# Dilated-attention scores on 128 rows, in column halves of 64 queries

## The chip, the cores and the metric

One core of a Trainium2 chip runs the whole program. The metric is the device time of one execution in microseconds (us), taken as the median of several runs. Besides, one execution was recorded by the hardware profiler; every duration below is from that one.

## What is computed

A hybrid encoder layer on two inputs, a "sample" of 1024 tokens and a "prompt" of 256 tokens, all in float32. Cut to what matters here:

```python
h = _rmsnorm(x, g_mix)
z = h @ w_in                      # queries, keys, values of both branches, gates
o_a = _banded_attention(qa, ka, va, A_WINDOW, 1, rel_bias[:, :A_HEADS], sink)
o_b = _dilated_mixture(qb, kb, vb, rel_bias[:, A_HEADS:])   # the branch that is changed
merged = gates0 * (o_a @ w_branch_a) + gates1 * (o_b @ w_branch_b)
x = x + merged @ w_out
y = _rmsnorm(x + square(relu(_rmsnorm(x, g_mlp) @ w_up)) @ w_down, g_final)
```

In the dilated branch there are three groups (window, dilation) = (128, 1), (512, 4), (2048, 16) of four heads, each head 64 wide. For every query the scores are `q . k / 8 + bias(distance)` over the keys of its window, then softmax and a sum over the values; the three groups are joined by their log-sums. The bias comes from a table of 32 buckets by heads.

## The kernel before, in words

The large products (`six`, L347; `mm3`, L191) are split by hand into high and low parts in the type float32r and use the full array: 128 rows of contraction by 128 columns of weights. The first stage projects the input. It runs over `PAIRS`, 14 pairs of 128 output columns; `pair` (L924) makes one of them with seven block products, and between pieces of about 12 matmuls it calls `tick` (L982). The small work of the dilated branch is laid between these pieces: every few ticks the generator `attention_b` (L489) makes one turn. The order of instructions on every engine is the order in which the code issues them (a manual schedule).

`BATCHES` (L475) cuts the dilated branch into 48 batches, by group and pair of heads. There are three kinds:

- 24 "wide" batches: one tile of 128 queries against 256 keys;
- 12 "double" batches: two tiles of 128 queries against 128 keys each;
- 12 "two-piece" batches: one tile whose first 64 queries and last 64 queries meet different stretches of 128 keys.

Turn j of `attention_b` issues, in this order (L581 to L590): the transposes of batch j-1 (L556), the values product of batch j-2 (L570), the scores of batch j (L537), the loads of values for j and of queries and keys for j+2 (L503, L505, on SP's queue). The first two turns have no values product, and the last two have no scores.

A batch covers two heads. Head 0 lies in partitions 0 to 63 of the tile `qk`, head 1 in partitions 64 to 127 (`HALVES`), so a scores matmul contracts over 64 rows: its weights are 64 rows by 128 queries (64 by 64 in a two-piece batch). The values product uses 128 rows by 64 columns: each half of the queries is a matmul of its own. Every plain float32 matmul shows as two instructions in the trace, each with its weight load. After the scores, VectorE adds the bias and takes the maximum (L541), and ScalarE the exponential (L545). `qk` has three buffers.

The generator `line` (L286) makes one row of bias for each of six cases: it loads a one-hot table of 33 rows on POOL's queue (L291), multiplies it with the bias table `tab` (33 rows by 20 heads, L295) into 256, 384 or 512 columns, and writes the result out over POOL's queue. Its steps are spread over a `pair` as hooks.

SP's queue also carries the weights of the next pair (`raw`, L377), the stores of finished pieces (L848) and the values (L519), all in the order of issue.

Of the kernel before, what the change touches and what calls it, by code (L numbers as in the profile page):

```python
# [10 lines left out]
F32 = mybir.dt.float32  # L11
# [4 lines left out]
P = 128  # L16
# [7 lines left out]
AH = 8  # L24
BH = 4
FF = 4 * D
EPS = 1e-6
NEG = -1e30
BUCKETS, MAXD = 32, 1024
# [20 lines left out]
HALVES = (slice(0, HD), slice(HD, P))  # L50
# [46 lines left out]
def encoder_kernel(  # L97
# [5 lines left out]
    nc = tc.nc  # L103
# [15 lines left out]
    const = ctx.enter_context(tc.tile_pool(name="const", bufs=1))  # L119
# [15 lines left out]
    def bank(tag, name=None):  # L135
        return psum.tile([P, 512], F32, name=name or tag, tag=tag, bufs={"mm": 3, "sc": 2, "pt": 2, "pv": 1}[tag])
# [115 lines left out]
    nc.vector.memset(eps, EPS)  # L252
    bg = const.tile([P, 2 * KC], F32, name="bg")
    nsink = const.tile([P, AH], F32, name="nsink")
    tab = const.tile([BUCKETS + 1, AH + 3 * BH], F32, name="tab")

    nm_a = const.tile([P, AH, NT], F32, name="nm_a")
    l_a = const.tile([P, AH, NT], F32, name="l_a")
# [12 lines left out]
    NH = AH + 3 * BH  # L271
# [14 lines left out]
    def line(i, make):  # L286

        h0, n, length, _ = LINES[i][3:]
        first = sum(x[5] for x in LINES[:i])
        hs = make("z")[: BUCKETS + 1, :length]  # L290
        nc.gpsimd.dma_start(hs, hot[:, first : first + length])  # L291
        yield
        yield
        ps = bank("pt", "line")
        nc.tensor.matmul(ps[:NH, :length], tab, hs, start=True, stop=True)  # L295
        ln = make("z")[:NH, :length]
        nc.vector.tensor_copy(ln, ps[:NH, :length])
        d = dram.tile([n, length], F32, name=f"line{i}")
        nc.gpsimd.dma_start(d, ln[h0 : h0 + n, :])
        wide = dram.tile([P, n, length], F32, name=f"wide{i}")  # L300
        nc.gpsimd.dma_start(wide, d[:, :].unsqueeze(0).to_broadcast([P, n, length]))
        lines[i] = wide
        yield
# [97 lines left out]
    scr_qb = [[dram.tile([P, T], F32, name=f"scr_qb{g}{i}") for i in range(2)] for g in range(3)]  # L401
    scr_kb = [[dram.tile([P, T], F32, name=f"scr_kb{g}{i}") for i in range(2)] for g in range(3)]
# [86 lines left out]
    def attention_b(make):  # L489

        n = len(BATCHES)
        held, rows, live, bias = {}, {}, {}, {}

        def load(j):

            if j >= n:
                return
            g, i, tiles = BATCHES[j]
            qk = held[j] = make("qk", (P, 4 * P), n=3)
            o = 0  # L500
            for t, (pieces, W, _) in tiles:
                for a, (p0, m, qa, ka) in enumerate(pieces):
                    nc.sync.dma_start(qk[:, o + p0 : o + p0 + m], scr_qb[g][i][:, qa : qa + m])  # L503
                    k = o + P + P * a
                    nc.sync.dma_start(qk[:, k : k + W], scr_kb[g][i][:, ka : ka + W])  # L505
                o += 2 * P
                if t == 0 or (g, t) == (1, 8):
                    bias[j] = load_bias_b(g, i, t, make)

        def load_v(j):  # L510
            if not 0 <= j < n:
                return
            g, i, tiles = BATCHES[j]
            v = rows[j] = make("v", (P, 2, P), n=3)
            o = 0
            for t, (pieces, W, _) in tiles:
                for a, (_, _, _, ka) in enumerate(pieces):
                    for k in range(W // P):
                        nc.sync.dma_start(v[:, o, :], values_rows(g, i, ka // P + k))  # L519
                        o += 1  # L520

        def scores(j):
            g, i, tiles = BATCHES[j]
            qk, nt = held.pop(j), len(tiles)
            whole, *flat = bias[max(x for x in bias if x <= j)]
            s = make("s", (P, 2, 2 * P))
            m = small.tile([P, 2, 2], F32, name="m", tag="m")
            o = make("o", (P, 2, ROW), n=4)
            banks = [bank("sc") for _ in range(2)]
            jobs = []  # L530
            for x, (t, (pieces, W, c0)) in enumerate(tiles):
                b = whole[:, :, c0 : c0 + W] if c0 is not None else flat[pieces[0][2] >= NS]
                for h in range(2):
                    ps, d = banks[h], HALVES[h]
                    for a, (p0, nq, _, _) in enumerate(pieces):
                        q, k = 2 * P * x + p0, 2 * P * x + P + P * a
                        nc.tensor.matmul(ps[p0 : p0 + nq, P * x : P * x + W], qk[d, q : q + nq],  # L537
                                         qk[d, k : k + W], start=True, stop=True)
                    jobs.append((s[:, h, P * x : P * x + W], ps[:, P * x : P * x + W], b[:, h, :], x, h))
            for d, src, b, x, h in jobs:  # L540
                nc.vector.tensor_tensor_reduce(d, src, b, 1.0, -3.0e38, op0=ALU.add, op1=ALU.max,  # L541
                                               accum_out=m[:, x, h : h + 1])
            nc.vector.tensor_scalar(o[:, :nt, 2 * HD : 2 * HD + 2], m[:, :nt, :], -1.0, None, op0=ALU.mult)  # L543
            for d, _, _, x, h in jobs:
                nc.scalar.activation(d, d, AF.Exp, bias=o[:, x, 2 * HD + h : 2 * HD + h + 1],  # L545
                                     accum_out=o[:, x, 2 * HD + 2 + h : 2 * HD + 3 + h])
            live[j] = s, o

        def transposes(j):
            g, i, tiles = BATCHES[j]  # L550
            s, o = live[j]
            pt = make("pt", (P, 4, P))
            ps = bank("pt")
            a = 2 * sum(W // P for _, (_, W, _) in tiles)
            for k in range(a):
                nc.tensor.transpose(ps[:, P * k : P * k + P], s[:, k % 2, P * (k // 2) : P * (k // 2) + P], ident)  # L556
            copy(pt[:, :a, :], ps[:, : P * a].rearrange("p (i q) -> p i q", q=P))
            live[j] = pt, o

        def values_of(j):  # L560
            g, i, tiles = BATCHES[j]
            (pt, o), v = live.pop(j), rows.pop(j)
            nt = len(tiles)
            pv = bank("pv")
            for x, (t, (pieces, W, _)) in enumerate(tiles):
                for h in range(2):
                    c = P * x + HD * h
                    for k in range(W // P):
                        for a, rows_ in enumerate(HALVES):
                            nc.tensor.matmul(pv[rows_, c : c + HD], pt[:, 2 * (x + k) + h, rows_],  # L570
                                             v[:, x + a * (len(pieces) - 1) + k, HALVES[h]],
                                             start=k == 0, stop=k == W // P - 1)
            copy(o[:, :nt, : 2 * HD], pv[:, : P * nt].rearrange("p (x c) -> p x c", c=P))
            for x, (t, (pieces, _, _)) in enumerate(tiles):
                for p0, nq, qa, _ in pieces:
                    nc.gpsimd.dma_start(scr_b[g][qa : qa + nq, i, :], o[p0 : p0 + nq, x, :])

        load(0)
        load(1)
        yield  # L580
        for j in range(n + 2):  # L581
            if 0 <= j - 1 < n:
                transposes(j - 1)
            if 0 <= j - 2 < n:
                values_of(j - 2)
            if j < n:
                scores(j)
            load_v(j)
            load(j + 2)
            yield  # L590
# [35 lines left out]
    with ExitStack() as pre:  # L626
# [115 lines left out]
        load_v(0, 3)  # L742
        for t in range(3, 6):
            load_x(t)
        nc.sync.dma_start(tab[:BUCKETS, :], rel_bias)
        nc.sync.dma_start(bg, b_gate[0].rearrange("(k p) -> p k", p=P))
        nc.sync.dma_start(nsink, sink[0].partition_broadcast(P))
        load_v(1, 0)
# [35 lines left out]
        scale(3)  # L784
        square(4)
        next(turns[2], None)
        nc.vector.memset(tab[BUCKETS:, :], NEG)
        nc.vector.tensor_scalar(nsink, nsink, -1.0, None, op0=ALU.mult)
        for t in range(2):
            evac(t, 0, pss[t])  # L790
# [2 lines left out]
        for t in range(2, NT):  # L793
# [13 lines left out]
            ps = bank("mm", "v")  # L807
# [18 lines left out]
        for t in (4, 5, 6, 7, 8, 9, 0, 1, 2, 3):  # L826
            ps = bank("mm", "v")
# [6 lines left out]
    if True:  # L834
# [15 lines left out]
        class Rows:  # L850
# [13 lines left out]
            def sum(self, t0, n, ps, other):  # L864
                out, a, b = self.views(t0, n, ps, other)
                nc.vector.scalar_tensor_tensor(out, a, self.scale, b, op0=ALU.mult, op1=ALU.add)
# [138 lines left out]
    if True:  # L1005
# [6 lines left out]
        tiles = []  # L1012
        for t in range(NT):
            s0, m = (0, 8) if t < 8 else (8, 2)
# [138 lines left out]
    if True:  # L1153
# [78 lines left out]
        for i in range(len(order) + 2):  # L1232
# [5 lines left out]
            if i < len(order):  # L1238
                u, t = order[i]
# [81 lines left out]
        for i, (x, b, c) in enumerate(jobs):  # L1321
            t0, n = BLOCKS[b]
# [17 lines left out]
            ps = bank("mm")  # L1340
# [4 lines left out]
            m, sg = mT.at(c, t0, n), sgs.pop(i)  # L1345
# [91 lines left out]
    with ExitStack() as pre:  # L1437
# [10 lines left out]
        p0 = []  # L1448
# [9 lines left out]
        for hh in range(2):  # L1458
            sl = slice(512 * hh, 512 * hh + 512)
            ws = [weight(0) for _ in range(4)]  # L1460
            for t in range(NT):
                m = m_parts.pop(t)
                ps = bank("mm")
# [47 lines left out]
    class Down:  # L1511
# [4 lines left out]
        def make(self, name, shape=(P, 2, 512), dt=F32):  # L1516
            return self.late.tile(list(shape), dt, name=name, tag="l4", bufs=8)
# [347 lines left out]
```

## Time and profile before

| | |
|---|---|
| median of 3 runs | 1723.61 us (1722.31 to 1723.79) |
| the profiled execution | 1725.24 us, of which the span of the instructions is 1723.4 us |
| TensorE (PE) busy | 1699.1 us, 99% of the span |
| TensorE weight loads (PEld) busy | 1427.9 us, 83% |
| VectorE (DVE) busy | 1004.2 us, 58% |
| ScalarE (ACT) busy | 711.5 us, 41% |
| GpSimd (POOL) busy | 413.8 us, 24% |
| DMA, mean | 149 GB/s |

Times within the span count from its start. Matmuls are pipelined and the durations of single ones overlap, so what a matmul costs is read from the distance between its start and the start of the next one, not from its duration. "x8" behind a row says that eight instructions in a row are merged in it.

### The profile page before, as it was taken

The page shows a single profiled execution, that of the slowest core. Times are in us where ns is not written, and L with a number is a line of the kernel's source. Part 1 is how long each engine was busy: PE and PEld are TensorE (multiplying, and loading weights), DVE is VectorE, ACT ScalarE, POOL GpSimd, SP SyncE. Part 2 cuts the span into 40 slices and gives each one's busy share as a digit, 9 for nine tenths or more (in the row PEclk, how much of TensorE's full clock was granted, in tenths as well). Part 3 has the DMA queues.
Part 4 walks back from the last instruction along what each step waited for, and adds up shares of the span by engine and source line. Part 5 has one row for each costly group of instructions (what it writes and reads, how often), then busy time and mean ns, then how long its engine had stood idle before and what let it go on. Part 6 is the DMA issues. An engine that isn't in the chain of part 4 may idle for free.

```text
span 1723.4 us, 26556 instructions
## 1 busy us (share of the span) xinstructions
PE 1699.1 (99%) x9952; PEld 1427.9 (83%) x9952; DVE 1004.2 (58%) x1719; ACT 711.5 (41%) x1519; POOL 413.8 (24%) x336
## 2 busy tenths in 40 slices
PE   7999999999999999999999999999999999999998
PEld 6898888888888788888888888888888888888886
DVE  5733454554453377577558655545456776667575
ACT  6232443444443356554357433333334333333344
POOL 0210111111101011100100255555555342314150
PEclk9999999999999999999999999999999999999999
DMA  6314655654444754375212344334437834533333
GB/s 238 121 48 123 175 151 176 189 178 139 135 124 134 231 153 132 117 262 196 75 62 86 109 133 156 134 118 138 156 125 244 307 126 162 208 116 116 116 116 123
DMA packets 234745, 256.36 MB, mean 149 GB/s; under 512 B 30447, under 2 KB 164675, under 8 KB 234488
## 3 DMA queue, kind: packets, MB, share of 16 engines
q1 hardware_dynamic: 226184, 232.32, 41.8%
q0 software_dynamic: 7344, 20.24, 3.6%
q10 hardware_dynamic: 1088, 2.10, 0.4%
q8 instruction: 79, 1.29, 0.3%
q14 instruction: 50, 0.41, 0.1%
HBM read 169.10 MB, written 90.73 MB: 151 GB/s over the span
## 4 chain that ended last, share of the span: by engine, by line
PE 93%; DVE 2%; DMA 2%; issue 1%; ACT 1%; POOL 0%; SPq 0%; DVEq 0%; ACTq 0%; POOLq 0%
PE dn L347 21%; PE x L347 19%; PE mm L191 14%; PE z L347 9%; PE v L724 6%; PE mm L347 5%; PE pv L347 5%; PE y L347 5%; PE pv L1066 2%; PE sc L537 2%; PE pv L570 2%; PE pt L1051 1%; PE pt L556 1%; PE tr L338 1%; PE sc L1028 1%
## 5 line engine op out<-in xcount | busy, mean ns | idle before, releaser
L347 PE MATMUL dn<-dhi,ulo 128*128 128x512 f32 x448 | 174.6, 390 | 2.1 <-DVE ulo L185 2.1
L347 PE MATMUL dn<-dhi,uhi 128*128 128x512 f32 x448 | 174.4, 389 | 0.0
L347 PE MATMUL dn<-dlo,uhi 128*128 128x512 f32 x448 | 174.4, 389 | 0.0
L347 PE MATMUL x<-chi,wlo 128*128 128x512 f32 x424 | 167.6, 395 | 0.0
L347 PE MATMUL x<-clo,whi 128*128 128x512 f32 x424 | 165.8, 391 | 0.0
L347 PE MATMUL x<-chi,whi 128*128 128x512 f32 x424 | 165.2, 390 | 0.0
L314 DVE TENSOR_TENSOR wlo<-ta,whi 128x1024 fp32r<-128x1024 f32 x30 | 54.5, 1817 | 167.7 <-ACT whi L312 153.6
L314 DVE TENSOR_TENSOR wlo<-raw,whi 128x1024 fp32r<-128x1024 f32 x60 | 88.8, 1480 | 104.8 <-ACT whi L312 104.8
L381 POOL TENSOR_TENSOR tb<-raw 128x512 f32<-128x512 f32 x16 | 20.7, 1295 | 346.3 <-DMA raw<-in_w_up_dram 213.1
L347 PEld LDWEIGHTS dn<-dhi,ulo 128*128 128x128 f32 x448 | 84.1, 188 | 20.4 <-DVE ulo L185 3.0
L185 DVE TENSOR_TENSOR ulo<-uraw,uhi 128x1024 fp32r<-128x1024 f32 x56 | 93.3, 1686 | 11.7 <-ACT uhi L184 11.7
L347 PEld LDWEIGHTS dn<-dhi,uhi 128*128 128x128 f32 x448 | 84.1, 188 | 17.5
L347 PEld LDWEIGHTS dn<-dlo,uhi 128*128 128x128 f32 x448 | 84.1, 188 | 17.3
L347 PEld LDWEIGHTS x<-chi,wlo 128*128 128x128 f32 x424 | 79.7, 188 | 18.7 <-issue 2.2
L347 PEld LDWEIGHTS x<-chi,whi 128*128 128x128 f32 x424 | 79.7, 188 | 17.0
L347 PEld LDWEIGHTS x<-clo,whi 128*128 128x128 f32 x424 | 79.8, 188 | 14.8 <-DVE clo L314 0.4
L545 ACT ACTIVATE s<-s,o 128x128 f32<-128x128 f32 (+1 forms) x120 | 52.3, 436 | 87.6 <-DVE o L543 56.5
L1701 DVE TENSOR_TENSOR v<-v,dn 128x512 f32<-128x512 f32 x90 | 59.5, 682 | 42.8 <-PE dn L347 38.5
L1550 POOL TENSOR_TENSOR t<-raw,t 128x1024 f32<-128x1024 f32 x16 | 46.6, 2932 | 144.9 <-DMA raw<-in_w_down_dram 144.9
L267 DVE COPY pt<-pt 128x512 f32<-128x512 f32 (+1 forms) x80 | 48.8, 610 | 51.0 <-PE pv L570 35.9
L347 PE MATMUL dn<-dhi,up 128*128 128x512 f32 x224 | 73.5, 389 | 0.0
L347 PE MATMUL z<-chi,wlo 128*128 128x512 f32 x184 | 72.3, 393 | 0.0
(341 smaller groups left out, 4650.1 us busy)
## 6 DMA issues: line engine op xcount, KB each, us to landing
scr_u<-u SPq DMA_DIRECT2D x112, 320.0 KB
uraw<-scr_u SPq DMA_DIRECT2D x56, 512.0 KB
raw<-in_w_in_dram SPq DMA_DIRECT2D x33, 512.0 KB
raw<-in_w_up_dram SPq DMA_DIRECT2D x32, 512.0 KB
raw<-in_w_down_dram SPq DMA_DIRECT2D x28, 512.0 KB
sg<-scr_g SPq DMA_DIRECT2D x32, 256.0 KB
uraw<-scr_u SPq DMA_DIRECT2D x28, 256.0 KB
v<-scr_v SPq DMA_DIRECT2D x96, 64.0 KB
```

The lines of the kernel that those rows point to most:

```text
L185: nc.vector.tensor_tensor(lo, src, hi.bitcast(F32), op=ALU.subtract)
L191: nc.tensor.matmul(ps, a, b, start=i == 0, stop=i == len(seq) - 1)
L267: nc.vector.tensor_copy(out, in_)
L314: nc.vector.tensor_tensor(lo, src, hi.bitcast(F32), op=ALU.subtract)
L347: nc.tensor.matmul(ps, a, b, start=first and i == 0, stop=last and i == len(seq) - 1, skip_group_check=True)
L537: nc.tensor.matmul(ps[p0 : p0 + nq, P * x : P * x + W], qk[d, q : q + nq], qk[d, k : k + W], start=True, stop=True)
L545: nc.scalar.activation(d, d, AF.Exp, bias=o[:, x, 2 * HD + h : 2 * HD + h + 1], accum_out=o[:, x, 2 * HD + 2 + h : 2 * HD + 3 + h])
L570: nc.tensor.matmul(pv[rows_, c : c + HD], pt[:, 2 * (x + k) + h, rows_], v[:, x + a * (len(pieces) - 1) + k, HALVES[h]], start=k == 0, sto ...
L724: nc.tensor.matmul(ps[:, :n], a, b, start=k == 0 and j == 0, stop=k == KC - 1 and j == 2)
L1066: nc.tensor.matmul(pv[rows_, HD * h : HD * h + HD], pt[:, 2 * b + h, rows_], src, start=b == 0, stop=b == W // P - 1)
L1550: nc.gpsimd.tensor_tensor(o, a, b, op=ALU.subtract)
L1701: nc.vector.tensor_tensor(v, v, ps, op=ALU.add)
```

## The change

In the dilated scores, the queries are loaded into tiles in which each head has its own 128-row block with the other head's 64 rows zero, and the keys stay together in a tile of their own. A scores matmul then contracts over all 128 rows (the zeros take out the other head), with the 64 queries of one column half as its weights, so each tile and head needs two matmuls, one for each half of the queries. The two tiles of queries (`apart0`, `apart1`) are filled with zeros once on POOL and used in turn; queries are loaded with one DMA for each head, so a tile has three loads where it had two (a two-piece tile six where it had four). Queries and keys have two buffers where `qk` had three. The bias table `tab` and its one-hot rows are padded with zeros to 128 rows, the table also to 128 columns; two more kinds of memset on POOL do it.

```diff
@@ constants
-    tab = const.tile([BUCKETS + 1, AH + 3 * BH], F32, name="tab")
+    tab = const.tile([P, P], F32, name="tab")
+    nc.gpsimd.memset(tab, 0.0)
@@ line
-        hs = make("z")[: BUCKETS + 1, :length]
-        nc.gpsimd.dma_start(hs, hot[:, first : first + length])
+        hs = make("z")[:, :length]
+        nc.gpsimd.memset(hs, 0.0)
+        nc.gpsimd.dma_start(hs[: BUCKETS + 1, :], hot[:, first : first + length])
...
-        nc.tensor.matmul(ps[:NH, :length], tab, hs, start=True, stop=True)
+        nc.tensor.matmul(ps[:, :length], tab, hs, start=True, stop=True)
@@ attention_b
+        apart = [make(f"apart{x}", (P, 2, 2, P)) for x in range(2)]
+        for x in apart:
+            nc.gpsimd.memset(x, 0.0)
@@ load
-            qk = held[j] = make("qk", (P, 4 * P), n=3)
-            o = 0
-            for t, (pieces, W, _) in tiles:
+            q, k = held[j] = apart[j % 2], make("k", (P, 2 * P), n=2)
+            for x, (t, (pieces, W, _)) in enumerate(tiles):
                 for a, (p0, m, qa, ka) in enumerate(pieces):
-                    nc.sync.dma_start(qk[:, o + p0 : o + p0 + m], scr_qb[g][i][:, qa : qa + m])
-                    k = o + P + P * a
-                    nc.sync.dma_start(qk[:, k : k + W], scr_kb[g][i][:, ka : ka + W])
-                o += 2 * P
+                    for h, d in enumerate(HALVES):
+                        nc.sync.dma_start(q[d, x, h, p0 : p0 + m], scr_qb[g][i][d, qa : qa + m])
+                    c = P * (x + a)
+                    nc.sync.dma_start(k[:, c : c + W], scr_kb[g][i][:, ka : ka + W])
@@ scores
-                    ps, d = banks[h], HALVES[h]
-                    for a, (p0, nq, _, _) in enumerate(pieces):
-                        q, k = 2 * P * x + p0, 2 * P * x + P + P * a
-                        nc.tensor.matmul(ps[p0 : p0 + nq, P * x : P * x + W], qk[d, q : q + nq],
-                                         qk[d, k : k + W], start=True, stop=True)
+                    ps = banks[h]
+                    for a, r in enumerate(HALVES):
+                        c = P * (x + a * (len(pieces) - 1))
+                        nc.tensor.matmul(ps[r, P * x : P * x + W], q[:, x, h, r], k[:, c : c + W],
+                                         start=True, stop=True)
```

Besides, the load of `tab` names its 20 columns, and the memset of its 33rd row names that row alone.

## Rows read from the trace of the kernel before

**Rows 1.** The page, part 1: busy time of each engine (share) xinstructions.
```profile
PE 1699.1 (99%) x9952; PEld 1427.9 (83%) x9952; DVE 1004.2 (58%) x1719; ACT 711.5 (41%) x1519; POOL 413.8 (24%) x336
```

**Rows 2.** The page, part 4: the chain that ended last, shares by engine.
```profile
PE 93%; DVE 2%; DMA 2%; issue 1%; ACT 1%; POOL 0%; SPq 0%; DVEq 0%; ACTq 0%; POOLq 0%
```

**Rows 3.** Windows: stretch, its length, busy time of each engine, PEclk, DMA, GB/s.
```profile
180.00:541.00 361.00, 361.00 (x2566) 295.10 (x2566) 181.56 (x468) 150.70 (x404) 47.92 (x86) 1.00 0.52 156
```

**Rows 4.** Timeline of TensorE over a double batch's turn: start, length, line, operation.
```profile
259.75 0.40 PE L347 MATMUL x<-chi,whi 128*128 128x512 f32 x1
259.99 0.60 PE L556 MATMUL pt<-ident,s 128*128 128x128 f32 x4
260.52 0.69 PE L570 MATMUL pv<-v,pt 128*64 128x64 f32 x16
261.13 0.71 PE L537 MATMUL sc<-qk 64*128 64x128 f32 x8
261.78 0.50 PE L347 MATMUL x<-chi,wlo 128*128 128x512 f32 x1
262.11 0.39 PE L347 MATMUL x<-clo,whi 128*128 128x512 f32 x1
262.34 0.40 PE L347 MATMUL x<-chi,whi 128*128 128x512 f32 x1
```

**Rows 5.** The same turn in windows so narrow that a row begins within a group.
```profile
260.62 0.40 PE L570 MATMUL pv<-v,pt 128*64 128x64 f32 x8
260.97 0.23 PE L570 MATMUL pv<-v,pt 128*64 128x64 f32 x2
261.46 0.39 PE L537 MATMUL sc<-qk 64*128 64x128 f32 x4
261.57 0.28 PE L537 MATMUL sc<-qk 64*128 64x128 f32 x2
```

**Rows 6.** Timeline of TensorE: scores of a wide batch, all, and its last two instructions.
```profile
270.03 0.70 PE L537 MATMUL sc<-qk 64*128 64x256 f32 x4
270.36 0.38 PE L537 MATMUL sc<-qk 64*128 64x256 f32 x2
...
270.67 0.50 PE L347 MATMUL y<-hhi,wlo 128*128 128x512 f32 x1
```

**Rows 7.** Timeline of TensorE: scores of a two-piece batch and the next matmul.
```profile
277.54 0.45 PE L537 MATMUL sc<-qk 64*64 64x128 f32 x8
277.92 0.51 PE L347 MATMUL x<-chi,wlo 128*128 128x512 f32 x1
```

**Rows 8.** Timeline of TensorE around one of the six bias lines.
```profile
254.69 0.39 PE L347 MATMUL x<-chi,whi 128*128 128x512 f32 x1
255.01 0.82 PE L295 MATMUL line<-z,tab 33*20 33x384 f32 x2
255.76 0.50 PE L347 MATMUL z<-hhi,wlo 128*128 128x512 f32 x1
256.10 0.39 PE L347 MATMUL z<-hlo,whi 128*128 128x512 f32 x1
```

**Rows 9.** Timeline of SP's queue in an earlier turn, and TensorE's scores there.
```profile
204.57 0.38 SPq L503 DMA_DIRECT2D qk<-scr_qb  x1
...
210.01 0.37 SPq L848 DMA_DIRECT2D scr_qb<-z  x1
...
206.55 0.72 PE L537 MATMUL sc<-qk 64*128 64x128 f32 x8
```

**Rows 10.** Waits of VectorE, 180 to 541: who waited for what, us, times, longest.
```profile
DVE tb L381 <- DMA raw<-in_w_in_dram: 2.9, 3, 1.2
```

**Rows 11.** Timeline of POOL at the start: a memset of 128 columns.
```profile
0.74 0.20 POOL masks.py:197 MEMSET ident<- 128x128 f32 x1 [0.29 <-POOLq L1852]
```

**Rows 12.** Waits of TensorE over the whole span: the two at the next stage's entry.
```profile
PE mm L191 <- DMA hhi<-scr_h: 1.7, 1, 1.7
PE mm L191 <- DMA hlo<-scr_h: 1.2, 2, 0.7
```

More of the change, by code (lines that the diff above doesn't have):

```diff
@@ L523, in scores @@
             g, i, tiles = BATCHES[j]
-            qk, nt = held.pop(j), len(tiles)
+            (q, k), nt = held.pop(j), len(tiles)
             whole, *flat = bias[max(x for x in bias if x <= j)]
@@ L744, in encoder_kernel @@
             load_x(t)
-        nc.sync.dma_start(tab[:BUCKETS, :], rel_bias)
+        nc.sync.dma_start(tab[:BUCKETS, : AH + 3 * BH], rel_bias)
         nc.sync.dma_start(bg, b_gate[0].rearrange("(k p) -> p k", p=P))
@@ L786, in encoder_kernel @@
         next(turns[2], None)
-        nc.vector.memset(tab[BUCKETS:, :], NEG)
+        nc.vector.memset(tab[BUCKETS : BUCKETS + 1, :], NEG)
         nc.vector.tensor_scalar(nsink, nsink, -1.0, None, op0=ALU.mult)
```

## The prediction

> **What bounds the kernel now.** I read the page's busy times first [rows 1]: TensorE is busy 99% of the span, the next engine 58%. Then the chain that ended last [rows 2]: it runs on TensorE for 93%. The change works between about 180 and 541 us, where the dilated turns lie, and the window over that stretch [rows 3] shows TensorE busy for all of its 361 us, at the full granted clock (1.00, the 2.4 GHz level), with VectorE busy for half of it. So there what TensorE has to do is the time: each ns added to or taken from its queue moves the end by one. What remains is to read what each kind of matmul takes of it, and for that the timeline of TensorE, start to start, because durations overlap [rows 4 to 8].
>
> **How a turn is spent.** A large matmul starts 0.23 us after the one before (262.11 to 262.34 [rows 4]), and the transposes follow one at about the same distance, 0.24 (259.75 to 259.99): same shape of array, nothing lost. Within the values product, instructions run in twos, one for each half of the columns: from 260.62 to 260.97 [rows 5] lie six such steps, so a step takes 0.06. In the double batch's scores a step (also two instructions, now the two heads, one on each half of the rows) takes 0.11 (261.46 to 261.57 [rows 5]).
>
> Where the shape changes, the distance is longer. From the last step of the values to the scores: 0.16 (260.97 [rows 5] to 261.13 [rows 4]). From the last scores step to the next large matmul: 0.21 with 128 columns (261.57 [rows 5] to 261.78 [rows 4]), 0.31 with 256 (270.36 to 270.67 [rows 6]). These lie on one line: 0.05 for every 64 columns streamed, and 0.10 that does not depend on them. The 0.10 is what a change of shape costs. Behind it the first weight load lies open: the first large matmul takes 0.33 (261.78 to 262.11 [rows 4]) in place of 0.23, so 0.10 to 0.11 for 128 columns of weights; the first step of the values takes 0.10 (260.52 to 260.62 [rows 4, 5]) in place of 0.06, so 0.05 for 64 columns. The wide batch agrees: its first step takes 0.33 (270.03 to 270.36 [rows 6]), 0.11 of load and 0.22 of streaming 256 columns.
>
> **The change, part by part.** All scores matmuls become 128 rows by 64 columns, the shape of the values product ahead of them. That removes one change of shape in each turn and the open load behind it. But the two heads shared a step before, each on its half of the rows; with the zeros each head takes the whole height, so now the two halves of one head's queries share a step, and the two heads need twice the steps. A step lasts as long as its columns of keys take to stream, and zeros are streamed like anything else.
>
> From the last values step to the next large matmul, then:
>
> - Wide batch. Before: 0.16 + 0.64 (270.03 to 270.67 [rows 6]) = 0.80. After: 0.06 from values to scores without a change of shape, four steps of 0.22 of which the last leaves with 0.31: 0.06 + 3 x 0.22 + 0.31 = 1.03. More by 0.23, 24 times: 5.5 us.
> - Double batch. Before: 0.16 + 0.65 (261.13 to 261.78 [rows 4]) = 0.81. After, eight steps in place of four: 0.06 + 7 x 0.11 + 0.21 = 1.04. More by 0.23, ten times: 2.3 us.
> - The first two turns are double batches with no values ahead: the change of shape stays, only the open load shrinks from 0.11 to 0.05. Before 0.65, after 0.05 + 8 x 0.11 + 0.10 = 1.03. More by 0.38, twice: 0.8 us.
> - Two-piece batch. Before, four instructions shared a step (two heads by two pieces), and it took 0.16 + 0.38 (277.54 to 277.92 [rows 7]) = 0.54. After: 0.06 + 3 x 0.11 + 0.21 = 0.60. More by 0.06, 12 times: 0.7 us.
>
> Together 9.3 us more.
>
> The bias lines gain. Around one of 384 columns the trace has 0.32 + 0.75 + 0.34 = 1.41 (254.69 to 256.10 [rows 8]). Padded to the full array it no longer changes the shape: 0.23 + 2 x 0.33 (384 columns at 0.22 for 256) + 0.23 = 1.12. Less by 0.29, which does not hang on the length, six times: 1.7 us less. Sum: 9.3 - 1.7 = **7.6 us more**.
>
> The rest I cost at nothing. The memsets: 128 columns take POOL 0.20 [rows 11], so a line's 256 to 512 columns under 0.8, and the line's matmul comes more than 10 us behind its load (the hooks lie several block products apart). The zeroing of the two query tiles costs as much twice, once, before the first load; if that cover were gone it is 1.6 us, once. SP issues 72 more loads at about 0.4 each [rows 9], 29 us spread over 361. With two buffers a load for batch j+2 must now wait until the scores of batch j have left the tile. In the turn shown, SP began that load at 204.57, ahead of the scores at 206.55; now it waits until 207.2, and six loads in place of four bring it to about 210.2. Behind it in the queue stand the store that went at 210.01, held by its own data anyway, and the next pair's weights. So it is a few tenths here, up to some 2 us where a weight load stands right behind. VectorE waits on such weights already [rows 10], 2.9 us in all, without TensorE ever waiting in this stretch [rows 3], so I take nothing and keep 0 to 4 us as its bounds.
>
> Other bounds: the 256-column step from 0.20 (twice 0.10, the difference of the two exits) to 0.23 (a large matmul's), over 72 steps: -1.4 to +0.7 us. The 128-column step from 0.10 to 0.12, over about 120: -1.2 to +1.2. At the entry to the next stage TensorE waits 2.9 us for transfers [rows 12]; if those did not move with it, up to 2.9 us would be absorbed. I take zero, since SP issues them behind stores that wait for TensorE's own results.
>
> **A rule that decides one term.** The 0.06 from values to scores has no row: nowhere before do two different products of the 128 by 64 shape follow each other. The nearest rows are the steps inside the values product, 0.06, and the change of shape, 0.16; I take the first, since the large matmuls and transposes, equal in shape, also follow at the ordinary distance. The Trainium skill, "TensorEngine Tiling (Array Packing)", section Key Properties, says that changing the tiling mode drains TensorE and changing the tile within a mode does not. By that rule the sum is the 7.6 us above; were the drain kept, it would be the first rival's. The trace agrees with its first half by the 0.10 at each change; the second half no run here shows for this pair of products.
>
> **The rivals.**
>
> 1. The drain between values and scores stays, so the change does not do what it says. Each of 46 turns keeps 0.10 and an open load of 0.05: 6.9 us on top, 14.5 more, 1738.1. For it: no row of that pair. Against: the transposes behind large matmuls.
> 2. The halves do not overlap in the scores: each step becomes two. Wide 0.06 + 7 x 0.22 + 0.31 = 1.91, double 0.06 + 15 x 0.11 + 0.21 = 1.92, two-piece 0.06 + 7 x 0.11 + 0.21 = 1.04: 24 x 1.11 + 10 x 1.11 + 12 x 0.50, the first two turns 2.5, less 1.7: 44.6 more, 1768. Against: the values product does just that overlap at 0.06 a step.
> 3. Faster: in column halves an instruction streams its keys once, not twice. The values step cannot tell, since a load of 64 columns (0.05) would also give 0.06. Then the steps are 0.11 and 0.06: wide 0.06 + 0.33 + 0.21 = 0.60, double 0.06 + 0.42 + 0.16 = 0.64, two-piece 0.06 + 0.18 + 0.16 = 0.40, the first two unchanged: 24 x 0.20 + 10 x 0.17 + 12 x 0.14 = 8.2 less, with the lines 9.9 less, 1713.7. It turns to slower as soon as a wide step is over 0.16. Against: the values leave with 0.16, on the line of the other exits; streamed once it would be 0.13.
> 4. SP becomes late: where the weights come later than VectorE's slack, sums and splits queue behind its wait and TensorE stops. Thirteen pairs at up to 1.7 us (four more loads): up to 22 more, some 1740 to 1753. Against: SP spends most of its time waiting for stores.
>
> **How the numbers follow.** The profiled execution took 1725.24, 1.6 above the median of the runs, so I add to the median: 1723.61 + 7.6 = 1731.2. Chances: forecast 0.77, rival 1 0.08, rival 2 0.04, rival 3 0.05, rival 4 0.04, and 0.02 that the next stage's waits absorb most of it. The forecast's own range is 1728 (absorbed waits, or short steps) to 1735 (long steps and a little of SP). To hold 8 in 10 with rival 1 in it: 1728 to 1739. About 0.2% (3.4 us) is what a measurement of this kernel can tell from no change. Slower by more: 0.90; within it: 0.05 (absorption, or a part of rival 3); faster: 0.05.
>
> **What would show it.** Right: scores rows of form 128*64, 480 instructions where there were 288, starting 0.06 behind the last values step; a wide batch with steps of 0.22 and 1.03 from values to the next large matmul, a double one 1.04; the bias line's neighbours at 0.23; TensorE still without waits between 180 and 541, and that stretch some 8 us longer. Wrong: 0.16 ahead of the scores (rival 1), steps of 0.44 or of 0.11 in a wide batch (2, 3), or waits of TensorE on splits or loads (4).

## The result, and the profile after

The change makes the kernel slower by 9.6 us: 1733.33 us (median of 4 runs, 1732.67 to 1734.76) against 1723.7 (4 runs, 1722.31 to 1725.87), a ratio of 1.0056 with a 95% interval of 1.0038 to 1.0073, that is 6.5 to 12.6 us more. A second time, with five runs, it was 1.0062 (1.0048 to 1.0077). The profiled execution took 1732.67 us with a span of 1730.8, 7.4 more than before.

The page's busy times of the changed kernel, which answer to [rows 1], and the window over the dilated turns, which answers to [rows 3] (they now end some 8 us later):

```profile
PE 1705.7 (99%) x10144; PEld 1435.3 (83%) x10144; DVE 1005.0 (58%) x1719; ACT 711.4 (41%) x1519; POOL 419.2 (24%) x345
...
180.00:549.00 369.00, 369.00 (x2751) 303.07 (x2751) 181.63 (x468) 150.48 (x403) 49.24 (x89) 1.00 0.52 153
```

TensorE has 192 instructions more and is still never idle in that stretch. The timeline of TensorE in the turn of the same double batch as in [rows 4], with one row from a narrow window within the scores:

```profile
260.29 0.39 PE L349 MATMUL x<-chi,whi 128*128 128x512 f32 x1
260.52 0.60 PE L560 MATMUL pt<-ident,s 128*128 128x128 f32 x4
261.05 0.69 PE L574 MATMUL pv<-v,pt 128*64 128x64 f32 x16
261.57 1.04 PE L541 MATMUL sc<-k,apart 128*64 128x128 f32 x16
...
262.33 0.28 PE L541 MATMUL sc<-k,apart 128*64 128x128 f32 x2
...
262.54 0.50 PE L349 MATMUL x<-chi,wlo 128*128 128x512 f32 x1
```

From the start of the values to the scores it is 0.52 us where it was 0.61 (260.52 to 261.13): the change of shape is gone. Then eight steps follow where there were four; the last begins at 262.33, so seven steps take 0.76, 0.11 each, and it leaves with 0.21. From scores to the next large matmul it is 0.97 where it was 0.65.

The same for a wide batch (answers to [rows 6]), a two-piece batch ([rows 7]) and a bias line ([rows 8]):

```profile
270.19 0.69 PE L574 MATMUL pv<-v,pt 128*64 128x64 f32 x16
270.70 1.04 PE L541 MATMUL sc<-k,apart 128*64 128x256 f32 x8
271.67 0.50 PE L349 MATMUL y<-hhi,wlo 128*128 128x512 f32 x1
...
278.48 0.61 PE L541 MATMUL sc<-k,apart 128*64 128x128 f32 x8
279.02 0.50 PE L349 MATMUL x<-chi,wlo 128*128 128x512 f32 x1
...
255.54 0.40 PE L349 MATMUL x<-chi,whi 128*128 128x512 f32 x1
255.77 0.81 PE L297 MATMUL line<-z,tab 128*128 128x384 f32 x2
256.13 0.69 PE L349 MATMUL z<-hhi,wlo 128*128 128x512 f32 x1
256.66 0.40 PE L349 MATMUL z<-hlo,whi 128*128 128x512 f32 x1
```

The wide batch's scores take 0.97 (0.64 before), the two-piece's 0.54 (0.38), and the way past the bias line 1.12 (255.54 to 256.66) where it was 1.41.

To have the sum of all this without what happens later, I measure one stretch in every profile: from the last `x<-clo,whi` ahead of the first bias line to the first `mm<-hhi,wlo` of the next stage. Its ends, first in the kernel before, then in the changed one:

```profile
136.30 0.39 PE L347 MATMUL x<-clo,whi 128*128 128x512 f32 x1
556.82 0.50 PE L191 MATMUL mm<-hhi,wlo 128*128 128x512 f32 x1
```

```profile
135.94 0.39 PE L349 MATMUL x<-clo,whi 128*128 128x512 f32 x1
564.32 0.50 PE L191 MATMUL mm<-hhi,wlo 128*128 128x512 f32 x1
```

420.52 us before, 428.38 after: 7.86 more. The prediction's sum was 7.6. The medians differ by some two us more than that. The interval of 6.5 to 12.6 still holds 7.86, so a further cost is not shown by this measurement; the experiments look for one.

### The profile page after: what moved, and what is told of

Same layout as the page of the kernel before. It is cut to its first block, busy times and chain, and to the rows that moved or that the text cites. A ratio compares the mean times of both kernels' runs of the same rounds, so it can differ in the third digit from the quotient of the medians.

```text
span 1730.8 us, 27114 instructions
## 1 busy us (share of the span) xinstructions
PE 1705.7 (99%) x10144; PEld 1435.3 (83%) x10144; DVE 1005.0 (58%) x1719; ACT 711.4 (41%) x1519; POOL 419.2 (24%) x345
## 4 chain that ended last, share of the span: by engine, by line
PE 93%; DVE 2%; DMA 2%; issue 1%; SPq 1%; ACT 1%; DVEq 0%; ACTq 0%
PE dn L349 21%; PE x L349 19%; PE mm L191 14%; PE z L349 9%; PE v L728 5%; PE pv L349 5%; PE y L349 5%; PE mm L349 5%; PE sc L541 2%; PE pv L1070 2%; PE pv L574 1%; PE pt L1055 1%; PE pt L560 1%; PE tr L340 1%; PE sc L1032 1%
## 5 line engine op out<-in xcount | busy, mean ns | idle before, releaser
L349 PEld LDWEIGHTS dn<-dlo,uhi 128*128 128x128 f32 x448 | 84.1, 188 | 17.3
L349 PEld LDWEIGHTS x<-chi,wlo 128*128 128x128 f32 x424 | 79.7, 188 | 19.4 <-issue 4.2
L349 PEld LDWEIGHTS x<-chi,whi 128*128 128x128 f32 x424 | 79.6, 188 | 17.1
L1705 DVE TENSOR_TENSOR v<-v,dn 128x512 f32<-128x512 f32 x90 | 59.5, 683 | 42.6 <-PE dn L349 37.9
```

The lines of the kernel that those rows point to most:

```text
L349: nc.tensor.matmul(ps, a, b, start=first and i == 0, stop=last and i == len(seq) - 1, skip_group_check=True)
L1705: nc.vector.tensor_tensor(v, v, ps, op=ALU.add)
```

## The experiments

All profiles give the stretch just defined; three kernels were profiled twice, and each gave the same stretch to the hundredth. The ratios carry the rest of the kernel too. A us figure worked out from a ratio is its distance from 1, times 1723.

| kernel | stretch, us | against before | ratio (95%) |
|---|---|---|---|
| before | 420.52 | | |
| changed | 428.38 | +7.86 | 1.0056 (1.0038 to 1.0073) |
| changed, again | 428.38 | +7.86 | 1.0062 (1.0048 to 1.0077) |
| lines alone | 418.62 | -1.90 | 0.9996 (0.9988 to 1.0005) |
| scores and loads alone | 430.26 | +9.74 | 1.0054 (1.0038 to 1.0070) |
| loads alone | 420.72 | +0.20 | 1.0007 (0.9997 to 1.0017) |
| changed, with an unused tile | 428.43 | +7.91 | 1.0045 (1.0032 to 1.0059) |
| lines, with an unused tile | 418.76 | -1.76 | 0.9983 (0.9974 to 0.9992) |
| the same again | 418.76 | -1.76 | 0.9985 (0.9976 to 0.9994) |
| before, moved by 416 bytes | 420.42 | -0.10 | 1.0013 (1.0004 to 1.0022) |
| changed, values ahead of transposes | 441.70 | +21.18 | one run, 1748.86 us |
| changed, heads ahead of halves | 430.27 | +9.75 | one run, 1737.86 us |
| lines and unused tile, scores in quarters | 417.18 | -3.34 | 0.9994 (0.9985 to 1.0003) |
| the same again | 417.18 | -3.34 | 0.9987 (0.9978 to 0.9995) |

### The changed kernel once more

No edit.

> The changed kernel once more, for a narrower interval and a second profile. The step count (theory A: steps doubled, one change of shape saved, bias lines cheaper) gives 7.6 us more than before. Rival B: the loads or queues add about 2 us on top, so 9.6 or more. If the entry of the next stage varies from one execution to the next by itself (rival C), this profile shows other waits at the stage's entry than the first one did, with the same gain of about 7.8 us up to 541 us.

The stretch is the same to the hundredth, so the sum of the steps repeats from one execution to the next. The time was 1734.85 us, 10.7 over before (8.3 to 13.3), and now the step sum lies outside the interval. That spoke for rival B or for something behind the dilated turns. Rival C holds too: TensorE's waits at the entry of the next stage were 1.6 and 0.7 us, where the first profile had 0.9 and 0.7, with the same stretch ahead of them.

### One part alone: lines, scores, loads

The lines alone: the hunks on `tab` and `line`, with the scores as before.

> Scores as before, only the bias table and its one-hot rows padded. Theory A: six lines at 0.29 us each, 1.7 us less than before, with the neighbours of a line at 0.23 us and no change of shape. Rival: the saved distance is taken back by a wait elsewhere, 0 us.

The scores and loads alone: the hunks on `attention_b`, with the lines as before.

> Scores and loads as changed, the bias lines as before. Theory A: 9.3 us more than before (24 wide batches at 0.23, ten double at 0.23, two at 0.38, 12 two-piece at 0.06). Rival B: 11 us or more, since the loads cost besides.

The loads alone: the new tiles and loads, but each head on its own half of the rows, and the lines as before (against the changed kernel, the scores' part of the edit):

```diff
+                    d = HALVES[h]
-                    for a, r in enumerate(HALVES):
-                        c = P * (x + a * (len(pieces) - 1))
-                        nc.tensor.matmul(ps[r, P * x : P * x + W], q[:, x, h, r], k[:, c : c + W],
+                    for a, (p0, nq, _, _) in enumerate(pieces):
+                        c = P * (x + a)
+                        nc.tensor.matmul(ps[p0 : p0 + nq, P * x : P * x + W], q[d, x, h, p0 : p0 + nq],
+                                         k[d, c : c + W], start=True, stop=True)
```

> The loads as changed (zeroed tiles used in turn, one load for each head, two buffers), but the scores contract over the 64 rows of their head as before, on the halves of the rows; bias lines as before. Theory A: 0 us, within 1 us either way, with no wait of TensorE between 180 and 541 us. Rival B: about 2 us more or above, with waits of SP's loads on the scores and of TensorE or VectorE behind them.

In the stretch the parts add up: -1.90 and +9.74 make 7.84. Scores and loads together gave 9.3 us over the whole kernel (6.5 to 12.1), theory A's figure. The loads move the stretch by 0.20 only, so rival B has little room there; over the whole kernel they gave +1.2 us (0.5 under to 2.9 over), which does not settle what they do behind the stretch. What SP does did change as the prediction said. Its queue's waits in the changed kernel, 150 to 560 us:

```profile
SPq L852 <- DVE z L908: 44.3, 14, 8.7
SPq L852 <- DVE z L870: 35.4, 11, 7.9
SPq L508 <- PE sc L541: 34.8, 19, 5.0
```

Before, the first two were 68.3 and 59.5 us, and the third 3.0. The loads now wait for the scores, and the stores behind them wait the less for their own data. VectorE's wait for the weights that come over this queue went from 2.9 us ([rows 10]) to 3.7 between 180 and 549 us, and TensorE has no wait in the stretch:

```profile
DVE tb L383 <- DMA raw<-in_w_in_dram: 3.7, 2, 2.0
```

The surprise is the lines: 1.90 us won in the stretch, and over the whole kernel 0.7 (2.1 under to 0.9 over), not told from zero. That interval holds 1.9 as well, so it is a hint that something behind the stretch takes the gain back, no more. In the profiles with padded lines by then, TensorE waited 1.4 to 1.7 us between 679 and 695 us, where the two branches are merged; it did not wait there in the kernel before, nor in the run with scores and loads:

```profile
PE pt L1055 <- DVE pt L268: 0.9, 1, 0.9
PE pt L1055 <- ACT s L1040: 0.5, 2, 0.3
```

These are of the changed kernel, 660 to 700. With the loads alone there was a small one at the same place:

```profile
PE pt L1054 <- DVE pt L267: 0.4, 1, 0.4
```

In the second profile of the changed kernel the clock fell to its half level (1.2 GHz) right behind these waits, for 3.4 us (granted 0.83 from 690 to 700 us); in the first it stayed at 1.00. VectorE's waits in the same stretch lead further back; the first row is of the kernel before, the other two are of the changed one:

```profile
DVE mm__7494 L1119 <- DMA r<-scr_b__83: 0.7, 1, 0.7
```

```profile
DVE mm__7673 L1123 <- DMA r<-scr_b__84: 1.9, 1, 1.9
DVE mm__7673 L1122 <- DMA r<-scr_b__83: 1.3, 1, 1.3
```

VectorE waits for the rows of the dilated branch that SP gathers there (`load_rows`), 528 bytes apiece. In the trace the packets of 528 bytes between 655 and 705 us took 29.1 ns on average before, 29.4 in the run with scores and loads and 30.0 with the loads alone, but 32.4 in the changed kernel and 32.8 with the lines alone. The median packet of an execution takes 28 ns in all of them; what differs is a slower part. Of all 7680 such packets, 166 took 32 to 47 ns before, and 1565 in the changed kernel. The lines have nothing to do with these rows. But in the compiled program the padded table takes 512 bytes of each partition where 96 were set aside, and every tile allocated behind it lies 416 bytes further.

### Position in the on-chip memory

The padded table with an unused tile behind it, so that the rest moves by 512 bytes:

```diff
     tab = const.tile([P, P], F32, name="tab")
+    const.tile([P, 20], F32, name="fill")
```

> The changed kernel with an unused tile of 20 columns behind the bias table, so that every tile behind it lies 512 bytes further than before, not 416. Theory D: the two us that the changed kernel loses behind 680 us come from the shift by 416 bytes (32 beyond a multiple of 64), which makes the 528-byte packets of the gathered rows slower, 32 in place of 28 ns. Then these packets are back at 28 ns, VectorE's wait for the rows and the 2.1 us of TensorE behind it are gone, and the time is 2 to 3 us under the changed kernel, some 8 over before. Rival E: the loss comes from the moved timing of the stage ahead; then nothing changes.

> Scores as before, only the bias table and its rows padded, with the same unused tile of 20 columns. Theory D: the 1.9 us that the lines gain up to 541 us are kept, so about 2 us less than before (1 to 4 less). Rival E: as without the tile, about 0.4 less.

The kernel before, with nothing but a move by 416 bytes:

```diff
     tab = const.tile([BUCKETS + 1, AH + 3 * BH], F32, name="tab")
+    const.tile([P, 104], F32, name="fill")
```

> The kernel before with an unused tile of 104 columns behind the bias table: every tile lies 416 bytes further, where the padded table puts it, and nothing else is changed. Theory D: 528-byte packets at 32 ns, a wait of TensorE of 1 to 2 us between 680 and 690 us, 1 to 3 us over before. Rival E: 0 us, no such wait.

All three came out by theory D in the times. With the unused tile the packets took 29.0 and 29.1 ns on average, as before (the 28 of the expectation is the median), and TensorE's wait at the merge was 0.07 us in all. VectorE's wait for the rows was not gone: 1.2 and 1.1 us were left, with no wait of TensorE behind them. The changed kernel then is 7.8 us over before (5.5 to 10.2), which is the sum of the steps. The lines alone, with the unused tile, are 2.9 us under before (1.4 to 4.5), faster than both kernels; a second measurement gave 2.6 under (1.0 to 4.1). The kernel before, only moved, loses 2.2 us (0.7 to 3.8), with the packets at 32.8 ns and the same waits in the same place. VectorE's there:

```profile
DVE mm__7495 L1120 <- DMA r<-scr_b__84: 1.5, 1, 1.5
DVE mm__7495 L1119 <- DMA r<-scr_b__83: 1.5, 1, 1.5
```

So the position is shown to be a cause by itself: same instructions, same stretch (0.10 apart), other addresses. TensorE's waits at the merge, 1.6 us here and none before, would make up most of the 2.2.

Why the address matters stays open. The gathered rows are not the only transfers that it changes: the packets of 256 bytes took 17.1 to 17.3 ns on average in every kernel without the move and 19.0 to 19.4 in every one with it. The Trainium skill, "DMA: Bandwidth & Descriptors", section How a descriptor splits into AXI transactions, says that a descriptor is cut at multiples of 256 bytes, and that one that begins in the middle fetches more than it needs. The compiled programs put a tile of six gathered rows 64 bytes beyond such a multiple before and 224 beyond it after. By that page an estimate for the six rows, 528 bytes apart, is 120 units of 32 bytes before and 118 after, though the first row alone goes from 19 to 24. The trace does not agree: the packets became slower, not equal, so the page's count, which is told of fetching and not of writing into a tile, does not explain them.

### The price of a change of shape

The changed kernel, with `values_of(j - 2)` called ahead of `transposes(j - 1)`:

> The changed kernel, with the values product ahead of the transposes in each turn, so that four changes of shape lie in a turn in place of two. Theory A: each costs 0.10 us and opens the weight load behind it (0.05 for 64 columns, 0.11 for 128), 0.36 us in each of 46 turns, 16 to 17 us more than the changed kernel by 541 us. Rival: a change of shape costs only where the scores stand, 8 us or less.

```profile
261.72 0.39 PE L349 MATMUL x<-chi,whi 128*128 128x512 f32 x1
262.04 0.69 PE L574 MATMUL pv<-v,pt 128*64 128x64 f32 x16
262.65 0.66 PE L560 MATMUL pt<-ident,s 128*128 128x128 f32 x4
263.24 1.09 PE L541 MATMUL sc<-k,apart 128*64 128x128 f32 x16
264.26 0.50 PE L349 MATMUL x<-chi,wlo 128*128 128x512 f32 x1
```

The stretch is 13.3 us longer than the changed kernel's, 0.29 for each of 46 turns. From a large matmul to the values it is 0.32 in place of 0.23 to the transposes; from the values to the transposes 0.61 in place of 0.52 to the scores; from the transposes to the scores 0.59; the scores take 1.02 in place of 0.97, since their first load is open again. So a change costs its 0.10 (here 0.09) at the two new places as well, and the rival that it costs only at the scores (8 us or less) falls. I expected 16 to 17 us: I had charged the transposes with an open load of 0.11, but behind the values they lose only about 0.06 (0.59 in place of the usual 0.53 from 259.99 to 260.52 in [rows 4]).

### The order of the halves

The changed kernel, with the two loops around a scores matmul exchanged:

```diff
-                for h in range(2):
-                    for a, r in enumerate(HALVES):
+                for a, r in enumerate(HALVES):
+                    for h in range(2):
```

> The changed kernel, with both heads of one column half issued ahead of both heads of the other half. Theory A (only neighbours in the order of issue share a step): a wide tile takes six steps in place of four, 0.43 us more, a double batch ten in place of eight, 0.22, a two-piece six in place of four, 0.22; 15 to 16 us more than the changed kernel by 541 us. Rival G: the halves overlap whatever the order, 0 us. If nothing overlaps any more, some 36 us.

Theory A falls here: 1.9 us in the stretch beyond the changed kernel, not 15. The scores of the wide batch, to be compared with 270.70 to 271.67 above, and two rows from narrow windows within them:

```profile
271.30 1.08 PE L540 MATMUL sc<-k,apart 128*64 128x256 f32 x8
...
271.52 0.59 PE L540 MATMUL sc<-k,apart 128*64 128x256 f32 x3
...
271.57 0.59 PE L540 MATMUL sc<-k,apart 128*64 128x256 f32 x3
...
272.31 0.50 PE L349 MATMUL y<-hhi,wlo 128*128 128x512 f32 x1
```

1.01 in place of 0.97. Eight instructions still take four steps of 0.22, so the two halves still overlap, one of them 0.05 behind the other (271.52 and 271.57), which shows once in each turn as 0.04 to 0.05 us. So what decides is that the work goes to different halves of the array, not that the matmuls are neighbours in the code. Whether the compiler or the engine brings them together is not shown.

### A faster form of the scores

Scores as before on the rows of their head, but each for 64 queries, on top of the lines with the unused tile:

```diff
-                    for a, (p0, nq, _, _) in enumerate(pieces):
-                        q, k = 2 * P * x + p0, 2 * P * x + P + P * a
-                        nc.tensor.matmul(ps[p0 : p0 + nq, P * x : P * x + W], qk[d, q : q + nq],
+                    for a, r in enumerate(HALVES):
+                        q, k = 2 * P * x + HD * a, 2 * P * x + P + P * a * (len(pieces) - 1)
+                        nc.tensor.matmul(ps[r, P * x : P * x + W], qk[d, q : q + HD],
```

> Padded bias lines and the unused tile of 20 columns, loads as before; every scores matmul contracts over the 64 rows of its head, for the 64 queries of one column half, so four share a step (two heads by two halves), as the two-piece batches do already. Theory A: steps stay as many as before, only the open load at the entry shrinks from 0.11 to 0.05 us in 36 turns, 1.9 us less than with whole columns, so 4 to 5 us less than before. Rival F: four do not overlap over 256 columns, each wide or double batch takes two to four steps more, 12 us or more over before.

> The same kernel as quarters_filled. Its gain of 3.3 us by the end of the dilated turns went at the entry of the last stage (about 1330 us), where TensorE waited 4.3 us for VectorE in place of 1.4 and ran at half the clock for 6.8 us. If that is a matter of the single execution (theory H), this profile has a shorter wait there, no half clock, and the median is 3 to 5 us under before. If it belongs to this kernel (rival I), the wait of 3 us or more is here again and the median is about 1 us under before.

> The same kernel as lines_filled, beside the other on the same chip: 2 to 4 us less than before, the wait at about 1330 us under 2 us as in its first profile. By theory H it is 1 to 2 us slower than the quarters; by rival I it is the faster one.

```profile
267.18 0.66 PE L540 MATMUL sc<-qk 64*64 64x256 f32 x8
267.77 0.50 PE L350 MATMUL y<-hhi,wlo 128*128 128x512 f32 x1
```

A wide batch's scores take 0.59 where [rows 6] has 0.64: four instructions share a step, and the open load is that of 64 columns. The stretch is 1.58 us shorter than with the lines alone, so rival F falls. But the whole kernel does not follow: 1.0 us (0.5 over to 2.6 under) and 2.2 us (0.9 to 3.8) under before, where the lines alone gave 2.9 and 2.6. Both its profiles lose the gain in one place, the entry of the last stage, here the wait and the window of the first one:

```profile
PE dn L350 <- DVE ulo L185: 4.3, 2, 3.3
...
1325.00:1345.00 20.00, 15.67 (x57) 12.11 (x56) 18.21 (x10) 8.07 (x13) 15.05 (x6) 0.83 0.59 211
```

Before, that wait was 1.4 us and the clock there 1.00; with the lines alone the wait was 1.2 and 1.7. Theory H, that it is a matter of the single execution, is not borne out by the second profile (4.5 us, clock 0.83 again); rival I expected a median about 1 us under before, and it was 2.2. The runs spread over 1718.6 to 1726 us, those of the lines with the tile over 1718.9 to 1722.8. Both profiled executions, 1724.33 and 1725.06 us, were among the slowest of their runs, so what the fast ones did at this place was not seen. Why VectorE is later there stays open, and so does which of the two is the better kernel.

## Why the prediction was right, and what it missed

**The bound** held: every us that the steps cost in the dilated turns was paid, since TensorE had no idle time there before and has none after.

**The saved change of shape** held: the scores start 0.09 earlier behind the values, rival 1 is out, and the price of a change was found again where four of them lie in a turn: 0.09 and an open load, 0.29 us a turn for the two more.

**The doubled steps** held: double batches 0.06 + 0.97 = 1.03 predicted as 1.04, wide ones 1.03 as 1.03, two-piece ones 0.60 as 0.60; scores and loads together +9.74 us where the sum said 9.3, 0.2 of it by the loads. Rival 2 would have shown in steps of twice the length and rival 3 in steps of half of it; neither is there.

**The bias lines** held in their place: 1.12 us past a line, as worked out, and 1.8 to 1.9 us for the six, predicted 1.7.

**SP's queue** (rival 4) held at nothing within 0.2 us of the stretch; the loads wait for the scores, as the prediction said, and TensorE waits for none of it.

**What was missed** is a term that stood in no step: that a wider table moves every tile behind it. It costs 2.2 us by itself (0.7 to 3.8), about what the lines gain. The prediction looked at the padding as work for POOL and as a shape for TensorE; it did not ask what else lies in the same memory. With the position put right the kernel is 7.8 us over before (5.5 to 10.2), where 7.6 was predicted; as changed, its time is 1733.33, 2.1 above the predicted 1731.2. The forecast's own range, 1728 to 1735, holds that time, but its upper part stood for long steps and for SP. That the missed term fits into it is luck.

**The entry of the next stage**, whose waits I left out of the sum and put in the range, gave some back in the first profile: TensorE waited there 0.9 and 0.7 us for the two transfers, where [rows 12] has 1.7 and 1.2, and the clock over the 10 us around them was granted at 0.83, where it was 0.66 before, that is 3.4 us at the half level (1.2 GHz) in place of 6.8:

```profile
573.00:583.00 10.00, 8.35 (x34) 6.20 (x33) 2.75 (x13) 2.21 (x6) 0.46 (x1) 0.83 0.93 307
```

```profile
567.00:577.00 10.00, 8.24 (x21) 6.01 (x22) 1.78 (x8) 2.04 (x5) 1.26 (x2) 0.66 0.84 275
```

In the other profiles the time at the half level at this place was anything from 0 to 6.8 us with the same instructions around it, so a single span says little about two us; the ratios of several runs and the stretch ahead of it do.

## What to carry to other kernels

A row-packed product of two 64-row heads gives up half its rate when zeros fill the rows; saving a change of shape (0.10 us here, and an open weight load of 0.11) pays for that only where the added steps are worth less than the saving. Here a turn saved 0.2 us and paid 0.43 (two more steps of 256 columns) or 0.44 (four more of 128). An estimate from these figures is that half the columns would break even; no run tried that. Measure a change on the engine that is full from one fixed instruction to another, and compare that with the whole: where the two differ, something outside the edit moved. And when a tile grows, look at what lies behind it: here a move by 416 bytes cost 2.2 us, and one by 512 bytes cost nothing that shows.

## What the runs showed of the hardware that I had not expected

- The address of a tile shows in the time: 416 bytes of shift made 528-byte packets take 32.8 ns in place of 29.1 on average (a slower part of them, the median stayed at 28), 256-byte packets 19.4 in place of 17.3, and the kernel 2.2 us slower.
- Matmuls on different halves of the array's columns overlap even when the code issues two of one half and then two of the other; the price was 0.04 to 0.05 us a turn.
- Four products on quarters of the array (64 rows by 64 columns) share a step of 256 streamed columns as well as two halves do: 0.59 us for a wide batch's scores against 0.64.
